# Issuing the output stores of a rotary-embedding kernel from GpSimd's software ring instead of ScalarE's hardware ring

## The chip, the cores and the metric

The kernel runs on one core of a Trainium2 chip. The metric is the device time of one execution in microseconds (us), lower is better. Every execution named here was in the fast state with a granted clock of 1.0. Three names recur. ACT is ScalarE, DVE is VectorE, POOL is GpSimd. A *ring* is the queue into which an engine puts the descriptors of a transfer (the entries that say what is to be moved); in the profiles the same 16 DMA engines serve all rings. The profile calls the rings of SP and ACT (q1 and q10) "hardware_dynamic" and that of GpSimd (q0) "software_dynamic"; below they are the hardware rings and the software ring.

## The reference

```python
# x: (16, 512, 1024) f32, 16 heads of 64; cos, sin: (512, 32) f32
x = x.reshape(batch, seq, num_heads, head_dim)
x1, x2 = x[..., :half_dim], x[..., half_dim:]
rotated = np.concatenate([x1 * cos - x2 * sin,
                          x1 * sin + x2 * cos], axis=-1)   # cos, sin broadcast over batch and heads
```

The input and the output are 33.55 MB each, and every element is used once.

## The kernel before

The input is taken in eight slabs of 4 MB. A slab is a tile of 128 partitions with 8192 f32 (32 KB) each, a partition's part being one contiguous run in memory. Five slab buffers exist. The SP engine issues the loads. A slab is worked on in two passes of 4096 columns: ACT casts f32 to bf16, DVE does two multiplies and one add, ACT casts the result back into the slab's own buffer. After the second pass ACT issues the store of the whole slab. The load that will use the buffer again waits until that store has landed.

```python
nb = 2; slots = 5; nslabs = batch // nb
...
def load(s):
    slab[s] = slabs.tile([P, W], f32, tag="slab", name="slab")
    nc.sync.dma_start(out=slab[s], in_=dram(x, s))
...
for i, src in enumerate((cos, sin)):                 # the tables: 64 KB each
    nc.gpsimd.dma_start(out=view(raw, ...), in_=bass.AP(tensor=src.tensor, ...))
...
cast(passes[0])
for i, u in enumerate(passes):                       # u = (slab, half)
    if i + 1 < len(passes):
        cast(passes[i + 1])                          # ACT, f32 -> bf16
    s, k = u
    xs, xu = slab[s], xb.pop(u)
    t2 = t2pool.tile([P, PW], bf16, tag="t2")
    for t, a in ((t2, rpp * hd), (xu, 0)):
        nc.vector.tensor_mul(out=t, in0=xu, in1=view(tab, ...))
    nc.vector.tensor_add(out=xu, in0=xu, in1=view(t2, ...))
    nc.scalar.copy(out=view(xs, k * PW, (1, PW)), in_=xu)      # bf16 -> f32
    if k == rpp // rows - 1:
        nc.scalar.dma_start(out=dram(out_flat, s), in_=xs)     # the store
        if s + slots < nslabs:
            load(s + slots)
```

Of the kernel before, what the change touches and what calls it, by code (L numbers as in the profile page):

```python
# [2 lines left out]

# [4 lines left out]


@with_exitstack  # L10
def kernel(
    ctx: ExitStack,
    tc: tile.TileContext,
    x: bass.AP,
    cos: bass.AP,
    sin: bass.AP,
    num_heads: int,
    out: bass.AP,
):
    nc = tc.nc  # L20
    P = nc.NUM_PARTITIONS

    batch, seq, dim = x.shape
    nh = num_heads
    hd = dim // nh
    half = hd // 2
    bf16 = mybir.dt.bfloat16
    f32 = mybir.dt.float32

    nb = 2  # L30
    slots = 5
    nslabs = batch // nb
    rpp = nb * seq // P
    W = rpp * dim
    SP = seq // rpp
    rows = 4
    PW = rows * dim
    TW = rpp * half

    out_flat = out.rearrange("b s h d -> b s (h d)")  # L40

    singles = ctx.enter_context(tc.tile_pool(name="singles", bufs=1))
    slabs = ctx.enter_context(tc.tile_pool(name="slabs", bufs=slots))
    tpool = ctx.enter_context(tc.tile_pool(name="tpool", bufs=3))
    t2pool = ctx.enter_context(tc.tile_pool(name="t2pool", bufs=2))
    psum = ctx.enter_context(tc.tile_pool(
        name="psum", bufs=1, space=bass.MemoryType.PSUM))


    def dram(t, s, a=0, n=W):  # L50
        return bass.AP(tensor=t.tensor, offset=t.offset + s * nb * seq * dim + a,
                       ap=[[W, P], [1, n]])


    def view(t, offset, *dims):
        return dataclasses.replace(t, offset=t.offset + offset,
                                   ap=[t.ap[0], *[list(d) for d in dims]])


    slab = {}  # L60
# [7 lines that stand above are left out]
    load(0)  # L68


    TR = seq // P
    G = rpp // TR
    raw = singles.tile([P, 2 * TR * half], f32, tag="raw")
    for i, src in enumerate((cos, sin)):
        nc.gpsimd.dma_start(out=view(raw, i * TR * half, (1, TR * half)), in_=bass.AP(  # L75
            tensor=src.tensor, offset=src.offset,
            ap=[[TR * half, P], [1, TR * half]]))

    for s in range(1, slots):
        load(s)  # L80


    pick = singles.tile([P, G * P], bf16, tag="pick")
    nc.gpsimd.memset(pick, 0.0)  # L84
    for g in range(G):
        part = view(pick, g * P, (SP, P // SP), (1, SP))
        nc.gpsimd.affine_select(  # L87
            out=part, in_=part, compare_op=mybir.AluOpType.not_equal, fill=1.0,
            base=-g, pattern=[[0, P // SP], [-G, SP]], channel_multiplier=1)

    tab1 = singles.tile([P, 2 * TR * half], bf16, tag="tab1")
    nc.vector.tensor_copy(out=tab1, in_=raw)  # L92
    acc = psum.tile([P, 2 * TW], f32, tag="acc")
    for i in range(2):
        for g in range(G):
            nc.tensor.matmul(view(acc, i * TW + g * TR * half, (1, TR * half)),  # L96
                             view(pick, g * P, (1, P)),
                             view(tab1, i * TR * half, (1, TR * half)),
                             start=True, stop=True)

    tab = singles.tile([P, 2 * rpp * hd], bf16, tag="tab")
    nc.vector.tensor_copy(out=view(tab, 0, (hd, 2 * rpp), (1, half)),  # L102
                          in_=view(acc, 0, (half, 2 * rpp), (1, half)))
    nc.vector.tensor_copy(out=view(tab, half, (hd, rpp), (1, half)),  # L104
                          in_=view(acc, 0, (half, rpp), (1, half)))
    nc.vector.tensor_scalar_mul(  # L106
        out=view(tab, rpp * hd + half, (hd, rpp), (1, half)),
        in0=view(acc, TW, (half, rpp), (1, half)), scalar1=-1.0)


    xb = {}


    def cast(u):
        s, k = u
        xb[u] = tpool.tile([P, PW], bf16, tag="xb", name="xb")
        nc.scalar.copy(out=xb[u], in_=view(slab[s], k * PW, (1, PW)))  # L117



    passes = [(s, k) for s in range(nslabs) for k in range(rpp // rows)]
    cast(passes[0])
    for i, u in enumerate(passes):
        if i + 1 < len(passes):
            cast(passes[i + 1])
# [4 lines that stand above are left out]
            nc.vector.tensor_mul(  # L130
                out=t, in0=xu,
                in1=view(tab, a + k * rows * hd, (hd, rows), (0, nh), (1, hd)))
        nc.vector.tensor_add(  # L133
            out=xu, in0=xu,
            in1=view(t2, half, (hd, rows * nh), (-half, 2), (1, half)))

        nc.scalar.copy(out=view(xs, k * PW, (1, PW)), in_=xu)  # L137
        if k == rpp // rows - 1:
            nc.scalar.dma_start(out=dram(out_flat, s), in_=xs)
            if s + slots < nslabs:  # L140
                load(s + slots)


# [1 line left out]
_INS = ['x', 'cos', 'sin', 'num_heads']  # L145
_OUTS = [((16, 512, 16, 64), 'float32')]

_NUMBERS = {'num_heads': 16}


# [26 lines left out]
```

## Time and profile before

| | before |
|---|---|
| time, median of the first three runs | 162.62 us |
| span of the profiled execution | 160.8 us |
| DMA queues' share of the span (loads, stores, tables) | 49.4%, 48.3%, 0.2% |
| ACT busy, DVE busy | 114.8 us, 111.3 us |

The lines below are from the profile page of the kernel before. They are, in order: the span; busy time by engine; DMA busy in tenths and throughput in 40 slices of the span; the queues with packets, MB and share of 16 engines' span; the chain of work that ended last; two groups of instructions with busy time, mean length in ns and idle time before them; and the issues with size and time from issue to landing.

```profile
span 160.8 us, 182 instructions
...
PE 0.6 (0%) x4; PEld 0.4 (0%) x4; DVE 111.3 (69%) x52; ACT 114.8 (71%) x33; POOL 2.3 (1%) x9
...
DMA  6999999999999999999999999999999999999993
GB/s 220 448 408 399 473 432 399 473 432 318 416 432 456 408 432 456 416 432 456 416 432 456 416 424 440 440 416 432 456 408 432 465 408 432 456 416 432 456 416 171
...
q1 hardware_dynamic: 1152, 33.55, 49.4%
q10 hardware_dynamic: 1152, 33.55, 48.3%
q0 software_dynamic: 64, 0.13, 0.2%
...
DMA 47%; ACT 25%; DVE 13%; issue 6%; ACTq 0%; SPq 0%
...
L117 ACT CAST xb<-slab 128x4096 bf16<-128x4096 f32 x16 | 57.5, 3602 | 27.1 <-DMA slab<-in_x_dram 27.1
L137 ACT CAST slab<-xb 128x4096 f32<-128x4096 bf16 x16 | 57.6, 3603 | 4.1 <-DVE xb L133 3.9
...
slab<-in_x_dram SPq DMA_DIRECT2D x8, 4096.0 KB, 27.1
out_dram<-slab ACTq DMA_DIRECT2D x8, 4096.0 KB, 28.9
```

The DMA line is the one to see first: 9 in every slice but the first and the last. The two hardware queues together hold the 16 engines for 97.7% of the span. ACT and DVE are busy for about 70%, and ACT's waits are mostly for loads, which themselves stand behind stores. Landing takes 27 to 29 us after issue, although the packets of 4 MB alone need 8 x 1.213 = 9.7 us of each engine, so every transfer has packets queued around it.

Next, the timeline of the kernel before, around one store and around the last (start, length, engine, line, operation).

```profile
48.47 3.60 ACT L117 CAST xb<-slab 128x4096 bf16<-128x4096 f32 x1
48.59 0.34 ACTq L139 DMA_DIRECT2D out_dram<-slab  x1
...
143.06 3.60 ACT L137 CAST slab<-xb 128x4096 f32<-128x4096 bf16 x1 [3.46 <-DVE xb L133]
146.70 0.34 ACTq L139 DMA_DIRECT2D out_dram<-slab  x1
```

"ACTq" is ACT's sequencer, the part of the engine that waits and issues. The issue of 0.34 us begins 0.12 us after a cast of 3.60 us has begun, and lies wholly under it.

### The profile page before, as it was taken

The page shows a single profiled execution, that of the slowest core. Times are in us where ns is not written, and L with a number is a line of the kernel's source. Part 1 is how long each engine was busy: PE and PEld are TensorE (multiplying, and loading weights), DVE is VectorE, ACT ScalarE, POOL GpSimd, SP SyncE. Part 2 cuts the span into 40 slices and gives each one's busy share as a digit, 9 for nine tenths or more (in the row PEclk, how much of TensorE's full clock was granted, in tenths as well). Part 3 has the DMA queues.
Part 4 walks back from the last instruction along what each step waited for, and adds up shares of the span by engine and source line. Part 5 has one row for each costly group of instructions (what it writes and reads, how often), then busy time and mean ns, then how long its engine had stood idle before and what let it go on. Part 6 is the DMA issues. An engine that isn't in the chain of part 4 may idle for free.

```text
span 160.8 us, 182 instructions
## 1 busy us (share of the span) xinstructions
PE 0.6 (0%) x4; PEld 0.4 (0%) x4; DVE 111.3 (69%) x52; ACT 114.8 (71%) x33; POOL 2.3 (1%) x9
## 2 busy tenths in 40 slices
PE   0010000000000000000000000000000000000000
PEld 0000000000000000000000000000000000000000
DVE  0003799999999999999997599907997099950000
ACT  3006939899999999999984999069990899744000
POOL 5000000000000000000000000000000000000000
DMA  6999999999999999999999999999999999999993
GB/s 220 448 408 399 473 432 399 473 432 318 416 432 456 408 432 456 416 432 456 416 432 456 416 424 440 440 416 432 456 408 432 465 408 432 456 416 432 456 416 171
DMA packets 2368, 67.24 MB, mean 418 GB/s; under 512 B 288, under 2 KB 288, under 8 KB 320
## 3 DMA queue, kind: packets, MB, share of 16 engines
q1 hardware_dynamic: 1152, 33.55, 49.4%
q10 hardware_dynamic: 1152, 33.55, 48.3%
q0 software_dynamic: 64, 0.13, 0.2%
HBM read 33.69 MB, written 33.55 MB: 418 GB/s over the span
## 4 chain that ended last, share of the span: by engine, by line
DMA 47%; ACT 25%; DVE 13%; issue 6%; ACTq 0%; SPq 0%
DMA slab<-in_x_dram 25%; DMA out_dram<-slab 22%; ACT slab L137 16%; ACT xb L117 9%; DVE xb L133 4%; DVE t L130 4%; DVE xb L130 4%; ACTq L137 0%; SPq L65 0%
## 5 line engine op out<-in xcount | busy, mean ns | idle before, releaser
L117 ACT CAST xb<-slab 128x4096 bf16<-128x4096 f32 x16 | 57.5, 3602 | 27.1 <-DMA slab<-in_x_dram 27.1
L137 ACT CAST slab<-xb 128x4096 f32<-128x4096 bf16 x16 | 57.6, 3603 | 4.1 <-DVE xb L133 3.9
L130 DVE TENSOR_TENSOR t<-xb,tab 128x4096 bf16<-128x4096 bf16 x16 | 36.7, 2291 | 18.8 <-ACT xb L117 18.4
L133 DVE TENSOR_TENSOR xb<-xb,t 128x4096 bf16<-128x4096 bf16 x16 | 36.7, 2292 | 0.5
L130 DVE TENSOR_TENSOR xb<-xb,tab 128x4096 bf16<-128x4096 bf16 x16 | 36.7, 2292 | 0.5
L92 DVE CAST tab<-raw 128x256 bf16<-128x256 f32 x1 | 0.3, 294 | 11.1 <-DMA raw<-in_sin_dram 11.1
L117 ACT ACT_TABLE_LOAD x1 | 1.3, 1283 | 0.7 <-PEq L158 0.7
L102 DVE CAST tab<-acc 128x512 bf16<-128x512 f32 x1 | 0.7, 692 | 0.7 <-PE acc L96 0.7
L75 POOL DMA_DIRECT2D raw<-in_cos_dram x1 | 0.7, 674 | 0.8 <-POOLq L158 0.8
L96 PE MATMUL acc<-tab,pick 128*128 128x128 bf16 x4 | 0.6, 302 | 11.5 <-DVE tab L92 11.5
L87 POOL TENSOR_SCALAR_AFFINE_SELECT pick<-pick 128x128 bf16<-128x128 bf16 x2 | 0.5, 290 | 0.1
L75 POOL DMA_DIRECT2D raw<-in_sin_dram x1 | 0.5, 537 | 0.0
L96 PEld LDWEIGHTS <-pick 128*128 128x128 bf16 x4 | 0.4, 128 | 11.4 <-issue 8.2
L104 DVE CAST tab<-acc 128x256 bf16<-128x256 f32 x1 | 0.4, 416 | 0.0
L106 DVE TENSOR_SCALAR tab<-acc 128x256 bf16<-128x256 f32 x1 | 0.4, 414 | 0.0
L84 POOL MEMSET pick<- 128x256 bf16 x1 | 0.3, 330 | 0.0
L158 POOL MEMSET const-float32-0.0<- 128x1 f32 x1 | 0.1, 100 | 0.2 <-issue 0.2
L158 POOL MEMSET const-bfloat16-1.0<- 128x1 bf16 x1 | 0.1, 103 | 0.0
L158 POOL MEMSET const-uint8-127<- 128x1 uint8 x1 | 0.1, 103 | 0.0
L158 POOL MEMSET const-float32-1.0<- 128x1 f32 x1 | 0.1, 100 | 0.0
## 6 DMA issues: line engine op xcount, KB each, us to landing
slab<-in_x_dram SPq DMA_DIRECT2D x8, 4096.0 KB, 27.1
out_dram<-slab ACTq DMA_DIRECT2D x8, 4096.0 KB, 28.9
raw<-in_cos_dram POOLq DMA_DIRECT2D x1, 64.0 KB, 7.1
raw<-in_sin_dram POOLq DMA_DIRECT2D x1, 64.0 KB, 9.1
```

Of the source, the lines that this page charges most:

```text
L75: nc.gpsimd.dma_start(out=view(raw, i * TR * half, (1, TR * half)), in_=bass.AP(tensor=src.tensor, offset=src.offset, ap=[[TR * half, P], ...
L84: nc.gpsimd.memset(pick, 0.0)
L87: nc.gpsimd.affine_select(out=part, in_=part, compare_op=mybir.AluOpType.not_equal, fill=1.0, base=-g, pattern=[[0, P // SP], [-G, SP]], c ...
L96: nc.tensor.matmul(view(acc, i * TW + g * TR * half, (1, TR * half)), view(pick, g * P, (1, P)), view(tab1, i * TR * half, (1, TR * half)) ...
L102: nc.vector.tensor_copy(out=view(tab, 0, (hd, 2 * rpp), (1, half)), in_=view(acc, 0, (half, 2 * rpp), (1, half)))
L104: nc.vector.tensor_copy(out=view(tab, half, (hd, rpp), (1, half)), in_=view(acc, 0, (half, rpp), (1, half)))
L106: nc.vector.tensor_scalar_mul(out=view(tab, rpp * hd + half, (hd, rpp), (1, half)), in0=view(acc, TW, (half, rpp), (1, half)), scalar1=-1.0)
L117: nc.scalar.copy(out=xb[u], in_=view(slab[s], k * PW, (1, PW)))
L130: nc.vector.tensor_mul(out=t, in0=xu, in1=view(tab, a + k * rows * hd, (hd, rows), (0, nh), (1, hd)))
L133: nc.vector.tensor_add(out=xu, in0=xu, in1=view(t2, half, (hd, rows * nh), (-half, 2), (1, half)))
L137: nc.scalar.copy(out=view(xs, k * PW, (1, PW)), in_=xu)
L158: nc = _bacc.Bacc("TRN2", target_bir_lowering=False, num_devices=1)
```

## The change

The store is issued by GpSimd, whose ring has so far carried only the two tables. It takes eight issues from ACT.

```diff
-            nc.scalar.dma_start(out=dram(out_flat, s), in_=xs)
+            nc.gpsimd.dma_start(out=dram(out_flat, s), in_=xs)
```

## The prediction

> **What bounds the kernel now.** The DMA engines. The slices of the span show DMA at 9 in all but the first and last. The queue table shows 33.55 MB on each of q1 (loads) and q10 (stores), 49.4% and 48.3% of 16 engines' span. By the packet records each engine moves 64 load and 64 store packets of 32,768 bytes, median 1213 ns: 128 x 1.213 = 155.3 us of the 160.8 us span. The rest is 1.7 us before the first load packet, 1.2 us after the last store packet (159.6), and slow packets at the start and at 35 to 39 us. ACT (114.8 us, 71%) and DVE (111.3 us, 69%) have slack; late in the kernel ACT waits for loads (27.1 us in the wait view), which share the engines with stores. The chain of waits agrees: 47% DMA.
>
> **What it removes.** Eight issues from ACT's sequencer, 0.34 us each. In the timeline each starts 0.12 us after the next cast began, and that cast keeps its 3.60 us: ACT gains nothing. Perhaps a one-off slow stretch goes: around the first store (issued 34.4, first packet 38.7) load packets took up to 2.67 us and a slice fell to 318 GB/s. If that belongs to the first use of ACT's ring, about 1.3 us is gained; if to the first write of the output, nothing.
>
> **What it adds.** Eight issues on GpSimd, 0.54 to 0.67 us each by the table loads, on an engine idle after 3.4 us; some tenths of a microsecond of latency per store, hidden behind queued packets: even the last store, issued at 146.7, finds the previous one running until 149.9.
> The Trainium skill, "SBUF — State Buffer", section "Who interferes with whom", warns that a two-port DVE instruction locks out GpSimd, and with it descriptor writing, but puts a two-input tensor multiply or add outside that. The 48 large DVE instructions are of that kind. No run yet shows it; I expect issues under 3 us.
>
> **What it moves.** Open is the ring's packet size. The Trainium skill, "DMA: Bandwidth & Descriptors", section "SWDGE vs HWDGE vs iDMA", prefers packets of at most 4096 bytes and says engines rotate between queues per packet. The tables' packets are 4096 bytes, 159 ns each. (a) If a 32 KB row stays one packet (65%), packets and sharing are as before. (b) If rows are cut into eight, a row costs 8 x 159 = 1272 ns, 59 more, times 64 rows: +3.8 us at most; loads then get up to eight times the stores' share and land earlier. I estimate that the engines stay fed.
>
> **On the critical path.** Only the DMA engines' total work, its start and its end. (a): -1.3 to +1 us. (b): +2 to +4 us.
>
> **Prediction.** 163.0 us, 80% range 161.3 to 166.5. Faster by over 2%: 0.02; within 2%: 0.86; slower by over 2%: 0.12.
>
> **What would show each step.** Queue table: 33.55 MB moved to the software queue; 1152 store packets under (a), about eight times as many under (b). DMA slices stay 9. ACT casts still 3.60 us. Eight GpSimd issues of 0.5 to 3 us. Last load landing near 124 us under (a), clearly earlier under (b).
>
> **What would make it wrong.** Descriptor writing held up by DVE (GpSimd issues of many microseconds, DMA slices below 9); software-ring packets slower than 1213 ns per row; a slow end of the program.

## The result, and the profile after

| | before | after |
|---|---|---|
| median (runs) | 162.65 us (4) | 162.84 us (4) |
| lowest to highest | 162.51 to 162.77 | 162.73 to 162.99 |
| ratio, 95% interval | | 1.0013 (0.9995 to 1.003) |

A ratio is the mean time of one kernel's fast runs over that of the other's from the same rounds, so it is not quite the ratio of the medians. The output is correct.

The same parts of the profile page after the change, with the new group of GpSimd issues:

```profile
span 160.9 us, 202 instructions
...
PE 0.6 (0%) x4; PEld 0.4 (0%) x4; DVE 111.3 (69%) x52; ACT 114.8 (71%) x33; POOL 6.6 (4%) x17
...
DMA  6999999999999999999999999999999999999993
GB/s 236 432 407 407 481 415 391 481 432 358 415 399 489 415 399 489 415 399 481 424 399 464 440 399 456 448 399 456 448 399 432 472 399 407 497 391 399 513 391 138
...
q1 hardware_dynamic: 1152, 33.55, 49.2%
q0 software_dynamic: 1216, 33.69, 48.5%
...
issue 81%; DMA 8%; POOL 2%; POOLq 0%
...
L117 ACT CAST xb<-slab 128x4096 bf16<-128x4096 f32 x16 | 57.5, 3602 | 27.5 <-DMA slab<-in_x_dram 27.5
L137 ACT CAST slab<-xb 128x4096 f32<-128x4096 bf16 x16 | 57.7, 3604 | 4.1 <-DVE xb L133 3.9
...
L139 POOL DMA_DIRECT2D out_dram<-slab x8 | 4.3, 540 | 140.3 <-ACT slab L137 140.3
...
out_dram<-slab POOLq DMA_DIRECT2D x8, 4096.0 KB, 27.9
```

The 33.55 MB of stores have moved from q10 to q0. The packets did not change: q0 now has 1216, which is its 64 of before plus the 1152 of q10. By the packet records the 1024 large ones are 32,768 bytes with a median of 1213 ns, as before. ACT's casts are as long as before, 3602 and 3604 ns. GpSimd was busy for 4.3 us more and idle for the rest, so eight issues of 540 ns are all that was added.

One line must not be taken at its word: "issue 81%" in the chain. That share is time for which the view found no releaser. The chain of this trace steps from one GpSimd issue to the one before it and does not connect the landings between them. The slices and the queue table still show what limits the kernel.

The timeline after the change, for the same store and the last one:

```profile
47.21 2.29 DVE L130 TENSOR_TENSOR xb<-xb,tab 128x4096 bf16<-128x4096 bf16 x1
48.42 3.60 ACT L117 CAST xb<-slab 128x4096 bf16<-128x4096 f32 x1
48.81 0.55 POOL L139 DMA_DIRECT2D out_dram<-slab  x1 [13.62 <-ACT slab L137]
...
143.59 3.60 ACT L137 CAST slab<-xb 128x4096 f32<-128x4096 bf16 x1 [3.42 <-DVE xb L133]
147.49 0.53 POOL L139 DMA_DIRECT2D out_dram<-slab  x1 [13.64 <-ACT slab L137]
```

ACT's cast still begins at 48.4 us, and a DVE multiply runs over the whole of the issue. The issue is later by 0.22 us and longer by 0.21 us. In both kernels the last store had to queue: it was issued at 146.7 and 147.5 us while the packets of the store before it ran on to 149.9 and 149.7 us. The last store packet ended at 159.60 us before and at 159.36 us after; the program then ended 1.22 us and 1.56 us later.

### The profile page after: what moved, and what is told of

It reads as the page before. It is cut to its first block, busy times and chain, and to the rows that moved or that the text cites. A ratio compares the mean times of both kernels' runs of the same rounds, so it can differ in the third digit from the quotient of the medians.

```text
span 160.9 us, 202 instructions
## 1 busy us (share of the span) xinstructions
PE 0.6 (0%) x4; PEld 0.4 (0%) x4; DVE 111.3 (69%) x52; ACT 114.8 (71%) x33; POOL 6.6 (4%) x17
## 3 DMA queue, kind: packets, MB, share of 16 engines
q1 hardware_dynamic: 1152, 33.55, 49.2%
q0 software_dynamic: 1216, 33.69, 48.5%
HBM read 33.69 MB, written 33.55 MB: 418 GB/s over the span
## 4 chain that ended last, share of the span: by engine, by line
issue 81%; DMA 8%; POOL 2%; POOLq 0%
DMA slab<-in_x_dram 8%; POOL out_dram L139 2%; POOLq L172 0%; POOLq L139 0%
## 5 line engine op out<-in xcount | busy, mean ns | idle before, releaser
L117 ACT CAST xb<-slab 128x4096 bf16<-128x4096 f32 x16 | 57.5, 3602 | 27.5 <-DMA slab<-in_x_dram 27.5
L137 ACT CAST slab<-xb 128x4096 f32<-128x4096 bf16 x16 | 57.7, 3604 | 4.1 <-DVE xb L133 3.9
L139 POOL DMA_DIRECT2D out_dram<-slab x8 | 4.3, 540 | 140.3 <-ACT slab L137 140.3
```

What stands on the lines that cost most here:

```text
L117: nc.scalar.copy(out=xb[u], in_=view(slab[s], k * PW, (1, PW)))
L139: nc.gpsimd.dma_start(out=dram(out_flat, s), in_=xs)
```

## The experiments

The first theory is that the DMA engines' total work sets the time, that the two rings are served alike, and that the software ring's own cost exists but is hidden behind queued packets. There were three rivals: the software ring costs nothing even when exposed; relieving ACT is a gain which the DMA limit hides; and DVE could hold up GpSimd's writing of descriptors, so that this kernel was only lucky. Kernels with paired names differ only in the engine that issues the store ("act" or "pool").

### One slab buffer: the store's latency exposed

With one buffer, load, compute and store of a slab follow each other.

```diff
-    slots = 5
+    slots = 1
-        if i + 1 < len(passes):
+        if i + 1 < len(passes) and passes[i + 1][0] == u[0]:
             cast(passes[i + 1])
                 load(s + slots)
+                cast(passes[i + 1])
```

> One slab buffer, so load, compute and store of a slab follow each other and nothing hides a store's latency; stores on ScalarE's ring. Per slab some 12 us load, 21 us from the first cast to the last, 12 us store, worked out from the times of before: about 360 us in all. It is the base for slot1_pool.

> The same with stores in the software ring. Theory (the software ring's extra cost exists, 0.2 to 1 us a store, and is hidden behind queued packets in the kernel of the change): 2 to 8 us slower than slot1_act, and the time from the last ScalarE cast of a slab to the first store packet longer by that much. Rival (the software ring costs no more than the hardware ring, so there was nothing to hide): within 1 us of slot1_act.

Measured: 358.29 us with ACT's ring and 363.24 us with the software ring (four runs each), 4.95 us more, 0.62 us a store. In the order of their instructions the two differ only in the issuing engine. The view of the stores, first of slot1_act, then of slot1_pool, with the issue's shortest, median and longest time in ns, and the time from issue to landing:

```profile
L139 ACTq DMA_DIRECT2D out_dram<-slab x8: 338/338/376, 34.6 to 344.2; - x8
...
DMA to landing us min/median/max: 11.1/11.1/11.2
```

```profile
L139 POOL DMA_DIRECT2D out_dram<-slab x8: 531/532/565, 34.7 to 348.4; - x8
...
DMA to landing us min/median/max: 11.3/11.4/11.4
```

The instruction and packet records give the parts, the same at every store after the first two within 0.02 us:

| | ACT's ring | software ring |
|---|---|---|
| end of ACT's cast to start of issue | 0.03 us | 0.29 us |
| start of issue to first store packet | 0.84 us | 1.10 us |
| sum | 0.87 us | 1.39 us |

So a store in the software ring starts 0.52 us later, half of it before the issue begins. That is most of the 0.62 us. Another 0.34 us, once in a run, lies between the last packet and the end of the program (see the last point of "Why the prediction was right"); some 0.4 us of the 4.95 were not traced. The Trainium skill, "DMA: Bandwidth & Descriptors", section "Latency and other measured facts", gives a first byte after about 600 ns for a hardware ring and about 1 us for the software ring. The direction agrees; 0.84 and 1.10 us are what this shows. The cost is real, and the kernel of the change hides nearly all of it: eight such delays would be 4.2 us, and its median is 0.2 us higher, with an interval of the ratio that includes no loss at all.

### Three loads left out: ACT on the critical path

The critical path is the chain of work whose end sets the time.

```diff
             if s + slots < nslabs:
-                load(s + slots)
+                slab[s + slots] = xs
```

The result is wrong: the last three slabs are computed from buffers that hold earlier results. The DMA engines are now busy for 88.2% of the span by the queue table of load5_act (53.5, 34.5 and 0.2), 128 of 145.7 us, and the chain of work that ended last is mostly ACT's (56%, against 25% before).

> The three loads after the first five are left out (wrong result on purpose: slabs 5 to 7 are computed from buffers that hold earlier results), so the DMA engines have 13 x 9.7 = 126 us of work and ScalarE's chain is the limit: 34.4 + 7 x 14.2 us to the last store's issue, then about 12 us: some 147 us. Stores on ScalarE's ring. Base for load5_pool.

> The same with stores in the software ring; ScalarE is now on the critical path. Theory (an issue of 0.34 us lies under the running cast and costs ScalarE nothing): within 0.5 us of load5_act, slower by some tenths for the last store's exposed latency. Rival (taking eight issues off ScalarE is a gain that the DMA limit hid in the first comparison): faster than load5_act by 8 x 0.34 = 2.7 us.

Measured: 147.92 and 148.86 us; the two ratios to before are 0.909 and 0.9147, so the software ring is 0.6% slower. The DMA slices late in the span show gaps, so the engines are no longer the limit there. The slices, the chain and the issues of load5_act, then the slices and the issues of load5_pool:

```profile
DMA  6999999999999999999999997996099609963993
...
ACT 56%; DVE 14%; issue 13%; DMA 9%; ACTq 0%
...
L139 ACTq DMA_DIRECT2D out_dram<-slab x8: 338/338/377, 34.3 to 133.5; - x8
```

```profile
DMA  5999999999999999999999996996099609963993
...
L139 POOL DMA_DIRECT2D out_dram<-slab x8: 533/533/567, 34.7 to 133.9; - x8
```

From the first issue to the last are seven slabs: 99.2 us in both, 14.2 us a slab. ACT's pace does not change by taking the issues away, which refutes the second rival (2.7 us faster). What is left is, in the profiled pair (0.80 us), the last store's exposed latency (0.52 us by the table above), the first slab, which was ready 0.13 us later in this trace, and the end of the program after the last packet (0.15 us longer). The measured 0.94 us is above the 0.5 us that was expected.

### Runs of 4 KB instead of 32 KB

Each store becomes two, one of the even and one of the odd 4 KB runs, so that runs cannot be merged.

```diff
-            nc.scalar.dma_start(out=dram(out_flat, s), in_=xs)
+            for odd in (0, 1024):
+                st = [(2048, 4), (1, 1024)]
+                nc.scalar.dma_start(
+                    out=bass.AP(tensor=out_flat.tensor,
+                                offset=out_flat.offset + s * nb * seq * dim + odd,
+                                ap=[[W, P], *[list(d) for d in st]]),
+                    in_=view(xs, odd, *st))
```

> Five buffers as before; each store is cut into two issues of 4 KB runs (even and odd runs of a row), on ScalarE's ring. The case (b) of the prediction: if packets follow the runs, a row costs more engine time (159 ns for 4 KB against 1213 for 32 KB: up to 59 ns a row, 3.8 us in all), loads get most of the engines while both queues are full, and the last load lands clearly before 124 us. Expected 164 to 167 us. Rival (packet size does not matter, or the sharing starves the stores): 162.7 or over 170.

> The same cut in the software ring. Theory (rings of the same packet size are shared and served alike): within 0.5% of row4k_act, store packets of 4096 bytes at about 157 ns in both, GpSimd issues longer than 0.54 us by the number of descriptors (512 runs against 128), perhaps 1 to 2 us. Rival (writing descriptors in software becomes the limit once there are several times as many): over 1% slower than row4k_act, with the DMA slices below 9.

Measured: 165.94 us (ratio to before 1.0202, 1.0154 to 1.0249, verdict unclear) and 167.64 us (1.0311, 1.0276 to 1.0345, verdict slower). The queue and the view of the stores, of row4k_act, then of row4k_pool:

```profile
q10 hardware_dynamic: 8448, 33.56, 49.6%
...
L141 ACTq DMA_DIRECT2D out_dram<-slab x16: 542/592/14293, 34.4 to 152.7; - x16
```

```profile
q0 software_dynamic: 8512, 33.69, 50.0%
...
L141 POOL DMA_DIRECT2D out_dram<-slab x16: 702/772/817, 34.5 to 142.0; - x16
```

Packets follow the runs in both rings: 8192 of 4096 bytes, median 159 ns, so that a row of eight costs 1272 ns against 1213. The last load landed at 118.5 and 119.3 us instead of 125.0. This is close to the case (b) of the prediction (with two issues for a store instead of one), and its size was +3.1 us with ACT's ring, as estimated, and +4.8 us with the software ring, above the "at most 3.8".

Two things were not expected. First, ACT's issues took up to 14.3 us, and ACT's next instruction had to wait for them, while no GpSimd issue took over 0.82 us. The timeline of row4k_act shows the two issues of one slab and the cast that came after them:

```profile
97.86 14.88 ACTq L141 DMA_DIRECT2D out_dram<-slab  x2
...
112.84 3.60 ACT L137 CAST slab<-xb 128x4096 f32<-128x4096 bf16 x1 [11.49 <-issue]
```

Here moving the issue does free ACT, by the 11.49 us of this one wait alone, and the time still does not improve: by the queue tables the DMA engines were busy for 98.3% of the span of row4k_act and 98.5% of that of row4k_pool, so that at most 2.8 us could be gained. Second, the software ring was 1.1% slower (1.0311 over 1.0202), which the theory had put within 0.5%. It is not descriptor writing as the rival had it: the issues stayed short. The profiled executions, with spans of 165.1 and 164.9 us, do not show the difference that the other runs show: the one of row4k_act was the slowest of its four (167.07 us) and the one of row4k_pool the fastest (166.93 us). So the cause stays open.

### Extra casts on VectorE, first form

```diff
+        if k == rpp // rows - 1:
+            for _ in range(2):
+                nc.vector.tensor_copy(out=t2, in_=view(xs, 0, (1, PW)))
         nc.scalar.copy(out=view(xs, k * PW, (1, PW)), in_=xu)
```

The prediction had set multiplies and adds apart from the DVE instructions that hold up GpSimd. Here two casts run on DVE around the store's issue.

> After the last add of each slab VectorE runs two extra casts of 128x4096 f32 to bf16 within SBUF (about 2.2 us each, their results are not used), so that one is running when the store is issued. Stores on ScalarE's ring: issues stay at 0.34 us. The compute stage is longer by up to 4.4 us a slab; as the DMA engines are the limit, the time should move by less than 3 us. Base for cast2_pool.

> The same with stores in the software ring. Theory (in the change the issues took 0.53 us beside multiplies and adds[...]): GpSimd issues or the waits before them grow by 0.5 to 2.2 us, time within 0.5% of cast2_act as the latency is hidden. Rival (VectorE holds up descriptor writing in no case here): issues stay at 0.53 to 0.57 us and start as long after the ScalarE cast as in the change.

Measured: 176.70 and 172.81 us. As a comparison of times this pair failed. DVE, busy for 146.5 and 143.2 us, became the limit (in cast2_act the chain that ended last lies on DVE for 82% of the span), so the expected "less than 3 us" was wrong, and the framework that orders the instructions gave the two kernels different orders on ACT and DVE, so the 3.9 us between them are not the ring's. It did give a clue. The timeline of cast2_pool at one store:

```profile
54.85 2.29 DVE L139 CAST t<-slab 128x4096 bf16<-128x4096 f32 x1
56.66 0.59 POOL L142 DMA_DIRECT2D out_dram<-slab  x1 [21.40 <-ACT slab L140]
```

The cast ends at 57.13 us (by the unrounded records), the issue 0.12 us after it. The other seven issues too ended 0.12 to 0.15 us after the cast that was running. The casts had only been near their ends, so that the issues looked almost normal (0.57 to 0.60 us, the last 0.84).

### One long VectorE instruction across the issue

To see whether that was chance, a long instruction was put on DVE in the one-buffer kernels, where DVE is idle between a slab's last add and the next slab. It runs far past the store's issue. The cut leaves out the edit of the one-buffer kernels; its comments mark what differs in slot1mul_pool.

```diff
+    long_in = singles.tile([P, 4 * PW], f32, tag="long_in")        # bf16 in slot1mul_pool
+    long_out = singles.tile([P, 4 * PW], bf16, tag="long_out")
+    nc.vector.memset(long_in, 0.0)                                 # and long_out in slot1mul_pool
...
+        if k == rpp // rows - 1:
+            nc.vector.tensor_copy(out=view(long_in, 0, (1, 1)), in_=view(xu, 0, (1, 1)))
+            nc.vector.tensor_copy(out=long_out, in_=long_in)
+            # slot1mul_pool: nc.vector.tensor_mul(out=long_out, in0=long_out, in1=long_in)
         nc.scalar.copy(out=view(xs, k * PW, (1, PW)), in_=xu)
```

> slot1_act with one long f32-to-bf16 cast (128x16384 within SBUF, about 9 us at the 2.29 us that 4096 elements took) on VectorE right after the last add of each slab, when VectorE would otherwise be idle; its result is not used. It runs from the last add to some 5 us past the end of ScalarE's last cast, so over the store's issue. Stores on ScalarE's ring: both theories say issues of 0.34 us, first packets 0.84 us after, a time within 1 us of slot1_act (358.3).

> The same with stores in the software ring. In cast2_pool every GpSimd issue ended about 0.12 us after the VectorE cast that was running. Theory (a two-port cast keeps GpSimd from writing descriptors until it ends): issues of about 5 to 6 us that end 0.12 us after the long cast, and a time of about 40 us (8 x 5) over slot1_pool (363.2). Rival (that was chance, the issue only took 0.06 us longer): issues of 0.53 to 0.6 us, time within 2 us of slot1_pool.

> The same place, stores in the software ring, but the long VectorE instruction is a bf16 multiply of two SBUF inputs (128x16384, about 9 us), the form of the kernel's own work. Theory[...]: issues of 0.53 us, time within 2 us of slot1_pool. Rival (any long VectorE instruction holds up the issue; in the change the multiplies were only short): issues of 5 us as with the cast.

| | first store's issue at | issue, median of eight | first packet after start of issue, median | time | against its slot1 kernel |
|---|---|---|---|---|---|
| slot1cast_act | 37.49 us | 0.34 us | 0.84 us | 361.36 us | +3.07 |
| slot1cast_pool | 37.76 us | 5.05 us | 5.61 us | 402.13 us | +38.89 |
| slot1mul_pool | 39.79 us | 0.53 us | 1.10 us | 368.27 us | +5.03 |

The memsets at the start delayed the tables, and with them the first store, by 2.9 us in the cast kernels (37.49 against 34.59) and by 5.1 us in the last (39.79 against 34.70); the expectations had forgotten that. With it taken off, slot1cast_act and slot1mul_pool stand as their base. Timelines at the first store of slot1cast_act, slot1cast_pool and slot1mul_pool:

```profile
33.99 8.69 DVE L143 CAST long_out<-long_in 128x16384 bf16<-128x16384 f32 x1
37.49 0.38 ACTq L146 DMA_DIRECT2D out_dram<-slab  x1
```

```profile
33.99 8.70 DVE L143 CAST long_out<-long_in 128x16384 bf16<-128x16384 f32 x1
37.76 5.04 POOL L146 DMA_DIRECT2D out_dram<-slab  x1 [34.35 <-ACT slab L144]
```

```profile
34.71 8.69 DVE L144 TENSOR_TENSOR long_out<-long_out,long_in 128x16384 bf16<-128x16384 bf16 x1
39.79 0.57 POOL L147 DMA_DIRECT2D out_dram<-slab  x1 [36.36 <-ACT slab L145]
```

With the cast, the software issue ended at 42.81 us, 0.12 us after the cast (42.69), and so at all eight stores. The cast kernels differ by 40.8 us; eight times the later first packet and later issue (5.61 - 0.84 + 0.26 = 5.03 us) are 40.2, and the later end of the program is 0.34 more. A multiply of the same length, 8.69 us, held nothing up. So it is the form of the DVE instruction that matters and not its length. What in the form was not separated: the cast has one input, of f32, and the multiply two, of bf16. The Trainium skill, "SBUF — State Buffer", section "Who interferes with whom", says that casts within SBUF can take the pair of ports that DVE shares with GpSimd, and that a two-input instruction was not seen to stall a transfer, for the inferred reason that it takes only the read port. These runs agree with what it says of both; the reason itself they do not test. ACT's ring showed no effect of the cast at all.

### A store at the very start

```diff
+    early = singles.tile([P, 128], f32, tag="early")
+    nc.vector.memset(early, 0.0)
+    nc.scalar.dma_start(out=dram(out_flat, 0, 0, 128), in_=early)
```

> Before, with one small store more (512 bytes a partition, zeros, overwritten later by the first slab's store) at the very start on ScalarE's ring. Where does the slow stretch at 35 to 39 us come from? If from the first use of the store ring or the first write of the output: the stretch is gone or moves to the start, load packets around 37 us take 1.21 us, time down by up to 1.3 us. If from the change from loads alone to loads and stores together: packets up to 2.2 to 2.7 us there again, time as before within 0.3 us.

Measured: 162.67 us, ratio 1.0 (0.9985 to 1.0015). Throughput in stretches (the last column, GB/s), of the kernel before, of the one after, and of early_act:

```profile
28.00:36.00 8.00, 0.00 (x0) 0.00 (x0) 7.90 (x5) 7.55 (x3) 0.00 (x0) 1.00 1.05 446
36.00:40.00 4.00, 0.00 (x0) 0.00 (x0) 3.62 (x2) 4.00 (x2) 0.00 (x0) 1.00 0.92 303
```

```profile
28.00:36.00 8.00, 0.00 (x0) 0.00 (x0) 7.90 (x5) 7.55 (x3) 0.57 (x1) 1.00 1.06 455
36.00:40.00 4.00, 0.00 (x0) 0.00 (x0) 3.62 (x2) 4.00 (x2) 0.00 (x0) 1.00 0.90 311
```

```profile
36.00:40.00 4.00, 0.00 (x0) 0.00 (x0) 3.62 (x2) 4.00 (x2) 0.00 (x0) 1.00 0.86 311
```

The dip from about 450 to some 300 GB/s is there in all three. It belongs neither to the first use of ACT's ring, since it stays with GpSimd's ring and after an early use of ACT's, nor to the first write of the output as a whole, since the early store had written to it (to 128 of its places; pages it did not touch are not excluded). What makes it was not found. The slow packets are those of loads (up to 2.67 us in the kernel before, while no store packet took over 1.23), and a store that begins beside running loads isn't enough. The small early store ran beside a load from 6 to 14 us, and throughput was 431 GB/s from 4 to 12 us against 430 in the kernel before; in row4k_act and row4k_pool throughput from 36 to 40 us was 419 and 410 GB/s, and slow load packets came later, at 50 to 53 us and at 68 us. In slot1_act the first load packets after each store were slow too (up to 2.38 us) with no store packet beside them. No version was found that beats both kernels: the engines are busy with 67 MB that reference and types demand.

## Why the prediction was right

The measured 162.84 us lies in the range of 161.3 to 166.5 and within 2% of before.

- **What bounds the kernel** was right. Both kernels have DMA at 9 in all slices between the first and the last, and store work of 77.6 us per engine in either ring.
- **ACT gains nothing** was right, and shown with ACT on the critical path: 14.2 us a slab with either ring.
- **The software ring's latency is hidden** was right. "Some tenths of a microsecond per store" measured 0.52 us more from the end of ACT's cast to the first packet. It cost 0.6 us a store with one buffer and nearly nothing with five.
- **Packet size, case (a)**, given 65%, came true: 1216 packets in q0, rows of 32,768 bytes. The figures for case (b) were tested as well: right for ACT's ring (+3.1 us), too low for the software ring (+4.8 us against "+3.8 us at most"), and that difference is not explained. The 167.64 us of row4k_pool lies above the stated range, so the number leans on (a) having held, which no run had shown when the prediction was made.
- **DVE does not hold up descriptor writing here** was right (issues of 0.53 us under a running multiply, the same as with DVE idle), and by the distinction that was given: the multiply does not, the cast does.
- **The slow stretch near 37 us** was left open by the prediction, between ACT's ring and the first write of the output. The first is refuted: the stretch is the same with either ring and after an early use of ACT's. The second does not hold for a small first write, and the cause stays open.
- **A slow end of the program** was named as a danger. The end after the last packet was 0.34 us longer (1.56 against 1.22), while that packet was 0.24 us earlier. The traces of the other kernels show that this belongs to the change: the end takes 1.22 to 1.23 us in five of the seven kernels with stores in ACT's ring (1.41 in load5_act, 1.45 in early_act), and 1.56 to 1.57 us in six of the seven with the software ring (1.88 in row4k_pool). Nothing hides it, since it comes after all packets; what makes it was not tested.

## What to carry to other kernels

Look first at whether the DMA engines are busy without a gap: then the ring of a transfer, and who issues it, changes little (0.1% here, and 1.1% with runs of 4 KB, for a reason that stays open), and neither a freed issue nor some tenths of latency showed in the time of this kernel. Where a store's latency is exposed, the software ring costs about half a microsecond more, and where VectorE runs a long cast within SBUF the issue lasts until the cast ends (5.05 us here). An issue on a busy compute engine is cheap while it lies under that engine's running instruction (0.34 us here), but check its length: with eight times as many runs it held ACT for up to 14 us.

## What the Trainium skill lacked or had wrong

- "SBUF — State Buffer", section "Who interferes with whom": nothing wrong was found, but the page has no figure for the two-input case. The runs give one: issues of 0.53 us under a multiply of 8.69 us, against 5.05 us under a cast of the same length.
- "DMA: Bandwidth & Descriptors", section "SWDGE vs HWDGE vs iDMA": packets of "≤4096 B preferably" could be read as if rows were cut. A contiguous row of 32,768 bytes stayed one packet of 1213 ns in the software ring; only smaller runs gave packets of 4096 bytes, 159 ns.
- The same page, section "Latency and other measured facts": it gives first bytes of about 600 ns and 1 us. Here the first packet came 0.84 and 1.10 us after the start of the issue, and the software issue itself began 0.26 us later after the ACT instruction that it waited for (0.29 against 0.03 us), which the section does not give.
- No page I read gives a figure for how long a hardware-ring issue can hold its engine's sequencer while earlier stores are in flight: up to 14.3 us for 512 runs of 4 KB, while the software ring's issues of the same runs stayed under 0.82 us.
- No page I read has the dip of throughput to 303 to 311 GB/s from 36 to 40 us, around the first store, in the kernels before and after and in early_act.
